# A fused decoder layer: its first projection taken 512 columns at a time, half of the weight remainders moved to GpSimd, and one softmax cut in two

## The chip, the cores and the metric

The kernel runs on one core of a Trainium2 chip. A time is the device time of one execution in microseconds (us). The engines are TensorE (PE; its weight loads are the row PEld), VectorE (DVE), ScalarE (ACT), GpSimd (POOL) and SyncE (SP), which here only issues DMAs. Each engine takes its instructions in program order and waits where an operand or a buffer is not ready.

## What is computed

One decoder layer over 256 tokens of width 2048, in float32:

```
xn = rms_norm(x);  proj = xn @ w_in                 # 2048 x 5696
o_nsa = gates * (compressed + selected + window attention)      # 16 heads
o_fox = attention with a forgetting bias                        # 16 heads
h = x + [rms_norm(o_nsa), rms_norm(o_fox)] @ w_out
h = h + sum over 32 experts of combine_e * (silu(hn@wg_e) * (hn@wu_e)) @ wd_e
out = rms_norm(h)
```

For the compressed branch, blocks of the projected columns `kcmp` and `vcmp` (512 columns together, called kcv here) go through a small MLP. Queries attend to the 15 blocks that come out.

## The kernel before

**Two parts.** For the first 470 us or so the core projects, attends, multiplies by `w_out` and routes. Then it streams the weights of all experts, 1 MB per DMA.

**Items.** `items` is the list of 1 MB weight blocks of the first part: 44 of `w_in`, then 16 of `w_out`. A block of `w_in` is 1024 rows by 256 columns, eight row chunks of 128, so two items make a projection of 256 columns. In order: kcv0, kcv1, v0, k0, v1, k1 (items 0 to 11), four query projections (12 to 19), then fq, fk and fv (20 to 43).

**hi and lo.** A product of float32 precision is made from rounded parts. `stream_conv(h)` splits half `h` of the items (two per item, 1024 elements per partition each): ACT writes `hi` (L190), then DVE writes `lo` = raw - hi (L191). The results lie in three buffers by turns, so half `h` can be split only when PE is done with half `h-3`. With `xh` and `xl` the parts of x, a projection takes `hi*xh`, `hi*xl` and `lo*xh`. `project` runs the first two as one matmul of 512 columns (`both`, or `xb(k)`), the third as one of 256, and adds the two accumulators at the end: an ACT copy (L321) and a DVE add (L322). `sum`, the result in SBUF, goes to `post`. The accumulators (`banks`, two PSUM banks each) are two by turns.

**The opening.** x arrives while items 0 and 1 (kcv0) run. Before chunk k the loop transposes block k+3 of x on PE (`x_chunk`, L294); ACT and DVE split it (L295, L296). From item 2 on `run_items` takes over.

**Background.** After each quarter of an item (two chunks) `run_items` makes one call of `background`: one step of the attention pipe, and one step of the first generator in `misc`. The generators of `misc` run in the order in which they were appended: `evac_kcv` (scales kcv into `kc2` with `row_scale`, L337), `gates`, then `compress`. `compress` first adds a vector to the blocks on POOL (`bk`, L481, 2 memsets and 8 adds), and in the same step starts the matmuls `bhc`. Later come `split_q_later` and `compressed`, once for each group of 8 heads. `compressed` makes `pcm`, the probabilities; four steps later PE transposes them (`bpt`, L744). `bpt` takes the PSUM bank that was used three takes before, by the scores `s_n` of an attention unit, so it waits until DVE has read those scores (L644).

Of the kernel before, what the change touches and what calls it, by code (L numbers as in the profile page):

```python
# [11 lines left out]
F32 = mybir.dt.float32  # L12
# [68 lines left out]
def tile_kernel(ctx: ExitStack, tc: tile.TileContext, a: dict, out):  # L81
# [33 lines left out]
    def mm(o, l, r, start, stop):  # L115
        pe.matmul(o, l, r, start=start, stop=stop, skip_group_check=True)  # L116
# [61 lines left out]
    def stream_conv(h):  # L178

        i, hf = divmod(h, 2)  # L180
        if i >= len(items):
            return
        nm, _, nk = items[i][:3]
        n2 = nk // 2
        cv = big.tile([P, n2, 2, 2048 // nk], F32R, tag=f"c{h % 3}", name=f"cv_{nm}_{hf}")
        hi, lo = cv[:, :, 0, :], cv[:, :, 1, :]
        r = raws[i][:, n2 * hf:n2 * hf + n2, :]
        n = n2 if h else n2 // 2
        for k in range(0, n2, n):
            act.activation(hi[:, k:k + n], r[:, k:k + n], AF.Copy)  # L190
            dve.tensor_tensor(lo[:, k:k + n], r[:, k:k + n], hi[:, k:k + n].bitcast(F32), ALU.subtract)  # L191
        halves[h] = cv

    def run_chunk(i, kk):
# [81 lines left out]
    def x_rows():  # L276
        for t in range(2):
            dve.tensor_scalar(oraw[0][:, 4, t * P:(t + 1) * P], ident, rsx[:, t:t + 1], None, ALU.mult)
        yield
        yield  # L280
        brs = bank("brs", "s")
        mm(brs[:, :T], onesq, oraw[0][:, 4, :], True, True)
        act.copy(rsb, brs[:, :T])
# [16 lines left out]
    def project(col, kind, name, post):  # L300
# [24 lines left out]
        for kg in range(2):  # L325
            items.append((f"{name}{kg}", w_in[kg * 1024:(kg + 1) * 1024, col:col + 256], 8,
                          lambda kk, hi, lo, both, kg=kg: chunk(kg, kk, hi, lo, both), end if kg == 1 else None))


    kc2 = []  # L330

    def row_scale(dst, src, f=None, s0=0):

        n, c, w = src.shape
        r = rsb[0:n, s0:s0 + w].unsqueeze(1).broadcast_to([n, c, w])
        if f is None:
            dve.tensor_tensor(dst, src, r, ALU.mult)  # L337
        else:
            dve.scalar_tensor_tensor(dst, src, f, r, ALU.mult, ALU.mult)

    def post_kcv(s_, i):
        kc2.append(ap_q.tile([P, 4, T], F32, tag="m6", name=f"kc2{i}", bufs=2))
        misc.append(evac_kcv(s_, i))
        if i == 1:
            misc.append(gates())
            misc.append(compress())

    def evac_kcv(s_, i):
        if i == 0:
            yield from x_rows()  # L350
            yield
            act.activation(w64h, w64, AF.Copy)
            dve.tensor_tensor(w64l, w64, w64h.bitcast(F32), ALU.subtract)
        yield
        kt = kc2[i]
        for gp in range(2):
            src = s_[64 * gp:64 * gp + 64]
            row_scale(kt[0:64, gp::2, :], src)
            row_scale(kt[64:128, gp::2, 0:T - 1], src[:, :, 1:T], s0=1)
            yield  # L360
# [192 lines left out]
    def pair_end(i, oT):  # L553

        if i < 8:
            G, j = divmod(i, 4)
            mm(oT[:, :T], vcbd[0][:, G, j, :], pTc[G], False, True)
        act.copy(oraw[i // 8][:, i % 8, :], oT[:, :T])
        part = i // 8
        if i % 8 == 0:  # L560
            pool.tensor_tensor(sq[:, part, :], oraw[i // 8][:, i % 8, :], oraw[i // 8][:, i % 8, :], ALU.mult)
        else:
            s2 = wk.tile([P, T], F32, tag="pcm", name=f"s2_{i}", bufs=1)
            pool.tensor_tensor(s2, oraw[i // 8][:, i % 8, :], oraw[i // 8][:, i % 8, :], ALU.mult)
            pool.tensor_tensor(sq[:, part, :], sq[:, part, :], s2, ALU.add)

# [139 lines left out]
    gb = gate.rearrange("p t (h b) -> p h t b", b=3)  # L706
    biases = {}

    def compressed(G, q):
        csc = bank(f"csc{G}", "s")  # L710
        for t in range(2):
            for r in range(4):
                o0 = (t * 4 + r) * 32
                mm(csc[:, o0:o0 + 32], q[:, r, t * P:(t + 1) * P],
                   kcd[:, 2 * G + r // 2].rearrange("p h c -> p (h c)"), t == 0 and r == 0, True)
        yield
        scs = wk.tile([P, 16, 16], F32, tag="scs", name=f"scs{G}", bufs=1)
        mx = wk.tile([P, 16], F32, tag="mx", name=f"mx{G}", bufs=1)
        ss = wk.tile([P, 16], F32, tag="ss", name=f"ss{G}", bufs=1)
        pcm = wk.tile([P, 2, P], F32, tag="pcm", name=f"pcm{G}", bufs=1)  # L720
        pool.memset(pcm, 0.0)
        scv = scs[:, :, 0:NBLK]
        for t in range(2):
            dve.tensor_tensor(scv[:, 8 * t:8 * t + 8],
                              csc[:, P * t:P * t + P].rearrange("p (u c) -> p u c", c=16)[:, :, 0:NBLK],
                              cb[:, t, 4 * G:4 * G + 4].rearrange("p r h c -> p (r h) c")[:, :, 0:NBLK], ALU.add)
        dve.tensor_reduce(mx, scv, AX.X, ALU.max)
        dve.tensor_scalar(mx, mx, -1e29, None, ALU.max)
        dve.tensor_tensor(scv, scv, mx.unsqueeze(2).broadcast_to([P, 16, NBLK]), ALU.subtract)
        yield  # L730
        act.activation(scv, scv, AF.Exp)
        yield
        dve.tensor_reduce(ss, scv, AX.X, ALU.add)
        dve.tensor_scalar(ss, ss, 1e-30, None, ALU.max)
        dve.reciprocal(ss, ss)
        dve.tensor_tensor(ss.rearrange("p (t h) -> p t h", t=2), ss.rearrange("p (t h) -> p t h", t=2),
                          gate.rearrange("p t (h b) -> p t h b", b=3)[:, :, 8 * G:8 * G + 8, 0], ALU.mult)
        dve.tensor_tensor(pcm.rearrange("p t (h c) -> p (t h) c", c=16)[:, :, 0:NBLK], scv,
                          ss.unsqueeze(2).broadcast_to([P, 16, NBLK]), ALU.mult)
        for _ in range(4):  # L740
            yield
        bpt = bank(f"bpt{G}", "s")
        for t in range(2):
            pe.transpose(bpt[:, t * P:(t + 1) * P], pcm[:, t], ident)  # L744
        pt = fp.tile([P, T], F32, name=f"pTc{G}")
        act.copy(pt, bpt[:, :T])
        pTc[G] = pt
        yield
# [11 lines left out]
    def post_q(s_, G, i):  # L760
        q = scaled
        evac_q(s_, q, i)
        if i == 0:
            qs2[G] = m8(f"m{2 + G}", f"q{G}", (4, 2, T), F32R)
            split_q(q, qs2[G], 0)
            return
        qs = qs2[G]
        misc.append(split_q_later(q, qs))
        misc.append(compressed(G, q))
        for j in range(4):  # L770
            p = 4 * G + j
# [280 lines left out]
    x_load(1024, D)  # L1052
    stream_dma(2)

    for i in range(2):
        post = items[i][4]
        if i:
            stream_dma(i + DMA_AHEAD)
        for kk in range(8):
            k = 8 * i + kk  # L1060
            if k == 0:
                x_chunk(0)
                x_chunk(1)
                stream_conv(0)
                x_chunk(2)
                stream_conv(1)
                stream_dma(3)
                sp.dma_start(csf, a["cst"][:, K_KEEP:K_W])
                early_loads()
            if k + 3 < 16:  # L1070
                x_chunk(k + 3)
            if k in (5, 8, 11, 13):
                n = (5, 8, 11, 13).index(k)
                square(n % 2, n // 2)
            if k == 14:
# [487 lines left out]
```

## Time and profile before

| | |
|---|---|
| time, median of 3 runs | 1428.51 us (1426.74 to 1428.99) |
| profiled execution | 1426.94 us, its span 1425.0 us |
| busy in the span | PE 1305.2 us (92%), DVE 510.8 (36%), ACT 328.3 (23%), POOL 80.0 (6%) |
| granted clock, mean | 0.991 |
| DMA | 479.94 MB, 337 GB/s over the span |

The clock is a share of full speed: 1.00 is the level of 2.4 GHz, 0.50 that of 1.2 GHz. Shares over the whole span mix two parts with different limits, so what a change in the first part does is read from that part.

### The profile page before, as it was taken

The page shows a single profiled execution, that of the slowest core. Times are in us where ns is not written, and L with a number is a line of the kernel's source. Part 1 is how long each engine was busy: PE and PEld are TensorE (multiplying, and loading weights), DVE is VectorE, ACT ScalarE, POOL GpSimd, SP SyncE. Part 2 cuts the span into 40 slices and gives each one's busy share as a digit, 9 for nine tenths or more (in the row PEclk, how much of TensorE's full clock was granted, in tenths as well). Part 3 has the DMA queues.
Part 4 walks back from the last instruction along what each step waited for, and adds up shares of the span by engine and source line. Part 5 has one row for each costly group of instructions (what it writes and reads, how often), then busy time and mean ns, then how long its engine had stood idle before and what let it go on. Part 6 is the DMA issues. An engine that isn't in the chain of part 4 may idle for free.

```text
span 1425.0 us, 16784 instructions
## 1 busy us (share of the span) xinstructions
PE 1305.2 (92%) x6758; PEld 733.7 (51%) x6758; DVE 510.8 (36%) x1013; ACT 328.3 (23%) x655; POOL 80.0 (6%) x95
## 2 busy tenths in 40 slices
PE   8999899999999999999998997997998899799885
PEld 6888688887787534334333442433433344243332
DVE  5656777767756304114113021220401212031022
ACT  5445556555545100100100000000000000000003
POOL 1200011131100003000000000000000000000003
PEclk9999999999999999999999999999999999999998
DMA  8655355655595899999999999999999999999994
GB/s 253 201 167 170 105 150 155 201 170 163 203 375 186 349 400 421 402 421 420 421 421 421 420 420 422 420 421 421 420 421 422 420 422 420 421 421 421 421 403 163
DMA packets 130772, 479.94 MB, mean 337 GB/s; under 512 B 14112, under 2 KB 69248, under 8 KB 82432
## 3 DMA queue, kind: packets, MB, share of 16 engines
q1 hardware_dynamic: 126320, 474.53, 85.0%
q10 hardware_dynamic: 4368, 4.27, 0.9%
q8 instruction: 55, 0.90, 0.3%
q14 instruction: 29, 0.24, 0.1%
HBM read 476.63 MB, written 2.14 MB: 336 GB/s over the span
## 4 chain that ended last, share of the span: by engine, by line
PE 50%; DMA 36%; DVE 7%; ACT 4%; issue 2%; SPq 0%; ACTq 0%; POOL 0%; DVEq 0%; POOLq 0%
DMA e_u<-in_expert_w_up_dram 14%; DMA e_d<-in_expert_w_down_dram 14%; PE bu L116 11%; DMA e_g<-in_expert_w_gate_dram 7%; PE bg L116 6%; PE wo L116 6%; PE by L116 6%; PE bo L116 3%; PE bx L116 2%; PE fq_ps L116 2%; PE fv_ps L116 2%; PE q_ps L116 2%; PE o L116 2%; PE v_ps L116 2%; PE fk_ps L116 2%
## 5 line engine op out<-in xcount | busy, mean ns | idle before, releaser
L116 PE MATMUL by<-e_d,hids 128*64 128x512 f32 (+2 forms) x1072 | 236.1, 576 | 32.5 <-DMA e_d<-in_expert_w_down_dram 31.8
L116 PE MATMUL bu<-e_u,xg 128*64 128x512 f32 x1024 | 242.4, 597 | 11.4 <-DMA e_u<-in_expert_w_up_dram 11.4
L116 PE MATMUL bg<-e_g,xg 128*64 128x512 f32 x1024 | 234.7, 596 | 12.7 <-DMA e_g<-in_expert_w_gate_dram 12.7
L1347 DVE TENSOR_TENSOR ys<-by,ys 128x512 fp32r<-128x512 f32 x60 | 40.0, 687 | 455.9 <-ACT ys L1346 455.1
L116 PEld LDWEIGHTS by<-e_d,hids 128*64 128x64 f32 x1072 | 79.9, 137 | 180.7 <-issue 117.1
L116 PEld LDWEIGHTS bg<-e_g,xg 128*64 128x64 f32 x1024 | 81.8, 137 | 142.9 <-issue 106.2
L116 PEld LDWEIGHTS bu<-e_u,xg 128*64 128x64 f32 x1024 | 78.7, 136 | 144.3 <-issue 112.7
L1361 DVE TENSOR_TENSOR y<-y,bo 128x512 f32<-128x512 f32 x112 | 71.9, 683 | 151.0 <-PE bo L116 151.0
L1346 ACT CAST ys<-by 128x512 fp32r<-128x512 f32 x60 | 35.2, 586 | 313.2 <-PE by L116 199.6
L116 PE MATMUL bo<-ys,scT 128*128 128x512 f32 x240 | 73.5, 427 | 13.3 <-ACT ys L1346 5.8
L116 PE MATMUL wo<-cv_wo,ohi 128*128 128x512 f32 x256 | 80.6, 396 | 0.0
L116 PEld LDWEIGHTS bx<-s,hh 128*128 128x128 f32 x512 | 63.7, 192 | 23.8 <-issue 13.0
L116 PE MATMUL bx<-s,hh 128*128 128x256 f32 x512 | 70.1, 290 | 4.6 <-DVE y L1361 2.9
L1275 DVE TENSOR_TENSOR xg<-bx,fw 128x512 f32<-128x512 f32 x64 | 43.5, 689 | 76.8 <-PE bx L116 76.8
L116 PEld LDWEIGHTS bo<-ys,scT 128*128 128x128 f32 x240 | 38.0, 188 | 60.1 <-issue 45.1
L1469 POOL TENSOR_TENSOR o<-y,e_fnw 128x256 f32<-128x256 f32 (+2 forms) x12 | 10.1, 866 | 836.2 <-DVE y L1382 836.2
L116 PEld LDWEIGHTS wo<-cv_wo,ohi 128*128 128x128 f32 x256 | 46.9, 188 | 10.4 <-issue 1.2
L1289 ACT CAST scT<-bsc 128x256 fp32r<-128x256 f32 x16 | 6.0, 372 | 193.8 <-PE bsc L116 193.8
L116 PE MATMUL fq_ps<-xhl,cv_fq 128*128 128x512 f32 (+1 forms) x256 | 50.5, 344 | 0.0
L1326 ACT COPY hids<-bh 128x512 f32<-128x512 f32 x16 | 9.4, 586 | 178.1 <-PE bh L1324 178.1
L116 PE MATMUL wo<-cv_wo,olo 128*128 128x512 f32 x128 | 50.0, 390 | 0.0
L1315 ACT ACTIVATE hids<-bg,c 128x512 f32<-128x512 f32 x16 | 11.0, 688 | 169.0 <-PE bg L116 169.0
(298 smaller groups left out, 1480.9 us busy)
## 6 DMA issues: line engine op xcount, KB each, us to landing
e_g<-in_expert_w_gate_dram SPq DMA_DIRECT2D x128, 1024.0 KB, 19.8
e_u<-in_expert_w_up_dram SPq DMA_DIRECT2D x128, 1024.0 KB, 19.8
e_d<-in_expert_w_down_dram SPq DMA_DIRECT2D x124, 1024.0 KB, 19.8
raw_wo<-in_w_out_dram SPq DMA_DIRECT2D x16, 1024.0 KB, 6.2
raw_q<-in_w_in_dram SPq DMA_DIRECT2D x8, 1024.0 KB, 5.3
raw_fq<-in_w_in_dram SPq DMA_DIRECT2D x8, 1024.0 KB, 5.2
raw_fk<-in_w_in_dram SPq DMA_DIRECT2D x8, 1024.0 KB, 5.2
raw_fv<-in_w_in_dram SPq DMA_DIRECT2D x8, 1024.0 KB, 5.3
```

Of the source, the lines that this page charges most:

```text
L116: pe.matmul(o, l, r, start=start, stop=stop, skip_group_check=True)
L1275: dve.tensor_tensor(xt_[:, i0:i0 + per, 0:m], bx.rearrange("p (i s) -> p i s", i=per), fw[:, 4 * j + i0:4 * j + i0 + per].unsqueeze(2).bro ...
L1289: act.copy(scT, bt[:, :T])
L1315: act.activation(hids[-1], bg_, AF.Silu, scale=c2[:, 1:2])
L1326: act.copy(hT, bh.rearrange("p (i s) -> p i s", i=4))
L1346: act.copy(hi, by[n])
L1347: dve.tensor_tensor(lo, by[n], hi.bitcast(F32), ALU.subtract)
L1361: dve.tensor_tensor(y[t][:, ns], base[t][:, ns], bo, ALU.add)
L1469: (dve if last else pool).tensor_tensor(o[t][:, ns], y[t][:, ns], fnw[:, ns], ALU.mult)
```

## The change

Three edits. (1) kcv is one projection of 512 columns (`project_first`): its items are 512 rows by 512 columns, four chunks each. Items 0 to 3 run inside the opening loop, one chunk per block of x. Each chunk takes 12 matmuls of 256 columns in place of 4 for half as many output columns. All three products add up in one accumulator, so the copy and the add at the end go away, and `evac_kcv` scales out of PSUM. (2) For the second half of each later item of `w_in` (`nk == 8`, 40 halves) `lo` is written on POOL. (3) `compressed` runs twice per group, for 4 heads each, the first half already after the group's first query projection. A buffer `s2` gets its own tag.

```diff
+        eng = pool if hf and nk == 8 else dve
         for k in range(0, n2, n):
             act.activation(hi[:, k:k + n], r[:, k:k + n], AF.Copy)
-            dve.tensor_tensor(lo[:, k:k + n], r[:, k:k + n], hi[:, k:k + n].bitcast(F32), ALU.subtract)
+            eng.tensor_tensor(lo[:, k:k + n], r[:, k:k + n], hi[:, k:k + n].bitcast(F32), ALU.subtract)
...
+    def project_first(col, name, post):
...
+            k = kg * 4 + kk
...
+            for ct in range(4):
+                o, cs = b[0][:, ct // 2, (ct % 2) * T:(ct % 2) * T + T], slice(ct * P, ct * P + P)
+                mm(o, hi[:, cs], xh(k), k == 0 and ct % 2 == 0, False)
+                mm(o, hi[:, cs], xl(k), False, False)
+                mm(o, lo[:, cs], xh(k), False, k == 15)
...
-    def post_kcv(s_, i):
-        kc2.append(ap_q.tile([P, 4, T], F32, tag="m6", name=f"kc2{i}", bufs=2))
-        misc.append(evac_kcv(s_, i))
-        if i == 1:
-            misc.append(gates())
-            misc.append(compress())
...
+    def post_kcv(b):
+        kc2.extend(ap_q.tile([P, 4, T], F32, tag="m6", name=f"kc2{i}", bufs=2) for i in range(2))
+        misc.append(evac_kcv(b))
+        misc.append(gates())
+        misc.append(compress())
...
+        for i in range(2):
+            kt = kc2[i]
+            for gp in range(2):
+                src = b[64 * gp:64 * gp + 64, i].rearrange("p (c t) -> p c t", c=2)
+                row_scale(kt[0:64, gp::2, :], src)
+                row_scale(kt[64:128, gp::2, 0:T - 1], src[:, :, 1:T], s0=1)
+                yield
...
-            s2 = wk.tile([P, T], F32, tag="pcm", name=f"s2_{i}", bufs=1)
+            s2 = wk.tile([P, T], F32, tag="s2", name=f"s2_{i}", bufs=1)
...
-    def compressed(G, q):
...
+    def compressed(G, q, i):
...
+        if i == 0:
+            return
...
+            misc.append(compressed(G, q, 0))
             return
         qs = qs2[G]
         misc.append(split_q_later(q, qs))
-        misc.append(compressed(G, q))
+        misc.append(compressed(G, q, 1))
...
-    for i in range(2):
+    for i in range(4):
         post = items[i][4]
         if i:
             stream_dma(i + DMA_AHEAD)
-        for kk in range(8):
-            k = 8 * i + kk
+        for kk in range(4):
+            k = 4 * i + kk
...
-            if kk % 4 == 0:
-                stream_conv(2 * i + 2 + kk // 4)
+            if kk % 2 == 0:
+                stream_conv(2 * i + 2 + kk // 2)
...
-    run_items(2, n_proj, at)
+    run_items(4, n_proj, at)
```

The order of the instructions before, on PE in the opening, from the transpose of block 3 of x on (`xt` are the transposes, `kcv_ps` the accumulator; chunks 0 and 1):

```order
L294 MATMUL xt_197<-cst,xs_85 128x128
L294 MATMUL xt_197<-cst,xs_86 128x128
L116 MATMUL kcv_ps<-xhl_114,cv_kcv_0_169 128x512
L116 MATMUL kcv_ps<-xhl_114,cv_kcv_0_169 128x256
L116 MATMUL kcv_ps<-xhl_114,cv_kcv_0_169 128x512
L116 MATMUL kcv_ps<-xhl_114,cv_kcv_0_169 128x256
L294 MATMUL xt_210<-cst,xs_85 128x128
L294 MATMUL xt_210<-cst,xs_86 128x128
```

And with the change, on PE at the same place:

```order
L295 MATMUL xt_197<-cst,xs_85 128x128
L295 MATMUL xt_197<-cst,xs_86 128x128
L116 MATMUL kcv_ps<-xhl_114,cv_kcv_0_169 128x256 x12
L295 MATMUL xt_218<-cst,xs_85 128x128
L295 MATMUL xt_218<-cst,xs_86 128x128
```

Between two pairs of transposes there are now 12 matmuls of 256 columns, where there were two of 512 and two of 256.

On POOL before, from the power that ends the norm of x (`rsx`) to the squares of the attention outputs (`sq`):

```order
L160 TENSOR_TENSOR rsx<-vx,neg_half 128x2
L1082 CAST lt<-csf 128x128
L1084 COPY fold<-cst 36x36 x2
L436 MEMSET gmem 16x127
L540 MEMSET kT_724 64x2048
L477 MEMSET bk 128x64
L481 TENSOR_TENSOR bk<-kc_352,vec 128x16x15 x4
L477 MEMSET bk 128x64
L481 TENSOR_TENSOR bk<-kc_451,vec 128x16x15 x4
```

On POOL with the change, from the fourth `lo` half (`cv_k`, item 7) to the one behind the adds:

```order
L192 TENSOR_TENSOR cv_k_1_649<-raw_k_498,cv_k_1_649 128x4x256
L192 TENSOR_TENSOR cv_v_1_732<-raw_v_546,cv_v_1_732 128x4x256
L455 MEMSET gmem 16x127
L559 MEMSET kT_760 64x2048
L192 TENSOR_TENSOR cv_v_1_794<-raw_v_600,cv_v_1_794 128x4x256
L496 MEMSET bk 128x64
L500 TENSOR_TENSOR bk<-kc_493,vec 128x16x15 x4
L496 MEMSET bk 128x64
L500 TENSOR_TENSOR bk<-kc_494,vec 128x16x15 x4
L192 TENSOR_TENSOR cv_k_1_872<-raw_k_692,cv_k_1_872 128x4x256
```

The eight `bk` adds stood behind nothing that waits for PE; now six `lo` halves stand ahead of them, the last of which (`cv_v_1_794`) is that of item 9.

On DVE with the change, from the `lo` of item 5's first half (`cv_v_0_500`) to the end of v0 (`v_sum`); `kc` is written from PSUM, and `cv_k_0_548` is the `lo` of item 6's first half:

```order
L192 TENSOR_TENSOR cv_v_0_500<-raw_v_349,cv_v_0_500 128x4x256
L279 TENSOR_SCALAR oraw_118<-cst,rsx 128x128 x2
L371 TENSOR_TENSOR w64hl<-gmem,w64hl 128x1024
L192 TENSOR_TENSOR cv_k_0_548<-raw_k_427,cv_k_0_548 128x4x256
L357 TENSOR_TENSOR kc_493<-kcv_ps,rsb 64x2x256
L357 TENSOR_TENSOR kc_493<-kcv_ps,rsb 64x2x255
L357 TENSOR_TENSOR kc_493<-kcv_ps,rsb 64x2x256
L357 TENSOR_TENSOR kc_493<-kcv_ps,rsb 64x2x255
L357 TENSOR_TENSOR kc_494<-kcv_ps,rsb 64x2x256
L357 TENSOR_TENSOR kc_494<-kcv_ps,rsb 64x2x255
L357 TENSOR_TENSOR kc_494<-kcv_ps,rsb 64x2x256
L357 TENSOR_TENSOR kc_494<-kcv_ps,rsb 64x2x255
```

All eight scalings now stand behind that `lo` half and read the accumulator `kcv_ps` itself; before, four stood one projection earlier, and all read a copy in SBUF.

## Rows read from the trace of the kernel before

**Rows 1.** Windows: us; then busy us of each engine, granted clock, DMA share, GB/s

```profile
core 0: us, PE busy (x) PEld busy (x) DVE busy (x) ACT busy (x) POOL busy (x), PEclk, DMA share, GB/s
8.50:27.75 19.25, 14.79 (x73) 12.28 (x73) 11.14 (x18) 12.68 (x23) 0.00 (x0) 0.82 1.03 294
27.75:42.44 14.69, 14.69 (x84) 12.70 (x84) 12.10 (x17) 8.75 (x13) 4.72 (x8) 1.00 0.73 224
...
128.24:160.00 31.76, 25.27 (x155) 21.77 (x154) 23.42 (x70) 17.20 (x43) 0.06 (x1) 0.89 0.42 125
160.00:300.00 140.00, 136.86 (x885) 116.08 (x884) 105.93 (x328) 83.86 (x213) 20.08 (x25) 1.00 0.53 162
300.00:400.00 100.00, 96.46 (x537) 78.78 (x537) 71.47 (x135) 51.96 (x98) 17.93 (x18) 1.00 0.57 190
```

**Rows 2.** The page's chain that ended last, shares of the span by line

```profile
DMA e_u<-in_expert_w_up_dram 14%; DMA e_d<-in_expert_w_down_dram 14%; PE bu L116 11%; DMA e_g<-in_expert_w_gate_dram 7%; PE bg L116 6%; PE wo L116 6%; PE by L116 6%; PE bo L116 3%; PE bx L116 2%; PE fq_ps L116 2%; PE fv_ps L116 2%; PE q_ps L116 2%; PE o L116 2%; PE v_ps L116 2%; PE fk_ps L116 2%
```

**Rows 3.** Timeline of PE in the opening: start, us, instruction, idle before, releaser

```profile
13.47 0.44 PE L294 MATMUL xt<-cst,xs 128*128 128x128 f32 x2 [1.64 <-DVE xhl L296]
...
16.45 0.69 PE L294 MATMUL xt<-cst,xs 128*128 128x128 f32 x2 [1.83 <-DVE xhl L296]
...
27.75 7.32 PE L116 MATMUL kcv_ps<-xhl,cv_kcv 128*128 128x512 f32 x40
...
42.44 5.82 PE L116 MATMUL v_ps<-cv_v,xhl 128*128 128x512 f32 x32
```

**Rows 4.** Timeline of PE at the experts' start, 16 matmuls of 256 columns

```profile
479.16 2.14 PE L116 MATMUL bx<-s,hh 128*128 128x256 f32 x16
```

**Rows 5.** The weights of v0: issue on SP's queue, and landing of the four

```profile
30.03 1.08 SPq L176 DMA_DIRECT2D raw_v<-in_w_in_dram  x2
...
DMA to landing us min/median/max: 5.4/7.6/10.3
```

**Rows 6.** One hi half on ACT (timeline), one lo half and one scaling on DVE (by form)

```profile
36.99 1.06 ACT L190 ACTIVATE cv_v<-raw_v 128x1024 fp32r<-128x1024 f32 x1
...
L191 DVE TENSOR_TENSOR cv_q<-raw_q,cv_q 128x1024 fp32r<-128x1024 f32 x16 | 19.4, 1222 | 7.1 <-ACT cv_q L190 7.0
L337 DVE TENSOR_TENSOR scaled<-k_sum,rsb 128x512 f32<-128x512 f32 x2 | 1.4, 692 | 0.1
```

**Rows 7.** POOL by form: adds and products of several widths, and the memsets of bk

```profile
L481 POOL TENSOR_TENSOR bk<-kc,vec 128x240 f32<-128x240 f32 x8 | 10.1, 1288 | 9.0 <-DVE kc L337 9.0
...
L1469 POOL TENSOR_TENSOR o<-y,e_fnw 128x512 f32<-128x512 f32 x4 | 5.0, 1278 | 831.4 <-DVE y L1382 831.4
L1469 POOL TENSOR_TENSOR o<-y,e_fnw 128x256 f32<-128x256 f32 x6 | 4.2, 727 | 4.5 <-DVE y L1382 4.5
...
L477 POOL MEMSET bk<- 128x64 f32 x2 | 0.5, 226 | 0.1
```

**Rows 8.** Timeline: first and last of the adds on POOL, PE around bhc

```profile
40.75 1.17 POOL L481 TENSOR_TENSOR bk<-kc,vec 128x240 f32<-128x240 f32 x1 [5.87 <-DVE kc L337]
...
51.10 3.07 POOL L481 TENSOR_TENSOR bk<-kc,vec 128x240 f32<-128x240 f32 x3 [1.34 <-DVE kc L337]
...
74.43 1.00 PE L116 MATMUL bcb<-tab,oh 128*128 128x64 f32 x8
75.24 1.64 PE L116 MATMUL v_ps<-cv_v,xhl 128*128 128x512 f32 x8
76.81 1.09 PE L116 MATMUL bhc<-oraw,bk 128*64 128x128 f32 x16
```

**Rows 9.** Timeline of POOL and DVE: a small DVE operation alone, and one beside POOL

```profile
132.69 0.17 DVE L648 TENSOR_SCALAR sm_n<-sm_n 128x4 f32<-128x4 f32 x1 [1.11 <-ACT pr_n L646]
...
256.10 1.30 POOL L794 TENSOR_TENSOR fb<-fb,csf 128x512 f32<-128x512 f32 x1
...
256.50 0.92 DVE L648 TENSOR_SCALAR sm_n<-sm_n 128x4 f32<-128x4 f32 x1 [1.11 <-ACT pr_n L646]
```

**Rows 10.** PE's longest wait (timeline), and windows of 1 us behind it

```profile
152.91 0.66 PE L744 MATMUL bpt<-cst,pcm 128*128 128x128 f32 x2 [6.49 <-DVE st_n L644]
...
154.00:155.00 1.00, 1.00 (x5) 0.89 (x4) 0.36 (x3) 1.00 (x5) 0.00 (x0) 0.50 0.05 16
155.00:156.00 1.00, 1.00 (x5) 0.85 (x4) 0.96 (x5) 1.00 (x3) 0.00 (x0) 0.69 0.00 0
156.00:157.00 1.00, 1.00 (x7) 0.86 (x6) 1.00 (x3) 0.23 (x1) 0.00 (x0) 1.00 0.00 0
```

More of the change, by code (lines that the diff above doesn't have):

```diff
@@ L327, in project, with chunk @@
                           lambda kk, hi, lo, both, kg=kg: chunk(kg, kk, hi, lo, both), end if kg == 1 else None))
+    def project_first(col, name, post):
+        b = []
+        def chunk(kg, kk, hi, lo, _):
+            k = kg * 4 + kk
+            if not b:
+                b.append(banks(f"{name}_ps"))
+            for ct in range(4):
[3 more added lines that the diff above has]
+                mm(o, lo[:, cs], xh(k), False, k == 15)
+        for kg in range(4):
+            items.append((f"{name}{kg}", w_in[kg * 512:(kg + 1) * 512, col:col + 512], 4,
+                          lambda kk, hi, lo, both, kg=kg: chunk(kg, kk, hi, lo, both),
+                          (lambda: post(b[0])) if kg == 3 else None))
     kc2 = []
@@ L339, in row_scale, with evac_kcv @@
             dve.scalar_tensor_tensor(dst, src, f, r, ALU.mult, ALU.mult)
-    def post_kcv(s_, i):
-        kc2.append(ap_q.tile([P, 4, T], F32, tag="m6", name=f"kc2{i}", bufs=2))
-        misc.append(evac_kcv(s_, i))
-        if i == 1:
-            misc.append(gates())
-            misc.append(compress())
[L348 to L353, printed above, removed]
-        yield
[L355 to L360, printed above, removed]
+    def post_kcv(b):
[3 more added lines that the diff above has]
+        misc.append(compress())
+    def evac_kcv(b):
+        yield from x_rows()
+        yield
+        act.activation(w64h, w64, AF.Copy)
+        dve.tensor_tensor(w64l, w64, w64h.bitcast(F32), ALU.subtract)
+        yield
[5 more added lines that the diff above has]
+                row_scale(kt[64:128, gp::2, 0:T - 1], src[:, :, 1:T], s0=1)
+                yield
     gate = fp.tile([P, 2, 48], F32, name="gate")
@@ L707, in tile_kernel @@
     biases = {}
-    def compressed(G, q):
-        csc = bank(f"csc{G}", "s")
+    pcms = {}
+    def compressed(G, q, i):
+        csc = bank(f"csc{G}{i}", "s")
         for t in range(2):
[L712 to L715, printed above, removed]
+            for r in range(2):
+                o0 = (t * 2 + r) * 32
+                mm(csc[:, o0:o0 + 32], q[:, 2 * i + r, t * P:(t + 1) * P],
+                   kcd[:, 2 * G + i].rearrange("p h c -> p (h c)"), t == 0 and r == 0, True)
         yield
[L717 to L721, printed above, removed]
+        if i == 0:
+            pcms[G] = wk.tile([P, 2, P], F32, tag="pcm", name=f"pcm{G}", bufs=1)
+            pool.memset(pcms[G], 0.0)
+        scs = wk.tile([P, 8, 16], F32, tag="scs", name=f"scs{G}{i}", bufs=2)
+        mx = wk.tile([P, 8], F32, tag="mx", name=f"mx{G}{i}", bufs=2)
+        ss = wk.tile([P, 8], F32, tag="ss", name=f"ss{G}{i}", bufs=2)
         scv = scs[:, :, 0:NBLK]
         for t in range(2):
-            dve.tensor_tensor(scv[:, 8 * t:8 * t + 8],
-                              csc[:, P * t:P * t + P].rearrange("p (u c) -> p u c", c=16)[:, :, 0:NBLK],
-                              cb[:, t, 4 * G:4 * G + 4].rearrange("p r h c -> p (r h) c")[:, :, 0:NBLK], ALU.add)
+            dve.tensor_tensor(scv[:, 4 * t:4 * t + 4],
+                              csc[:, 64 * t:64 * t + 64].rearrange("p (u c) -> p u c", c=16)[:, :, 0:NBLK],
+                              cb[:, t, 4 * G + 2 * i:4 * G + 2 * i + 2].rearrange("p r h c -> p (r h) c")[:, :, 0:NBLK],
+                              ALU.add)
         dve.tensor_reduce(mx, scv, AX.X, ALU.max)
         dve.tensor_scalar(mx, mx, -1e29, None, ALU.max)
-        dve.tensor_tensor(scv, scv, mx.unsqueeze(2).broadcast_to([P, 16, NBLK]), ALU.subtract)
+        dve.tensor_tensor(scv, scv, mx.unsqueeze(2).broadcast_to([P, 8, NBLK]), ALU.subtract)
         yield
@@ L735, in compressed @@
         dve.reciprocal(ss, ss)
[L736 to L739, printed above, removed]
+        sst = ss.rearrange("p (t h) -> p t h", t=2)
+        dve.tensor_tensor(sst, sst, gate.rearrange("p t (h b) -> p t h b", b=3)[:, :, 8 * G + 4 * i:8 * G + 4 * i + 4, 0],
+                          ALU.mult)
+        for t in range(2):
+            dve.tensor_tensor(pcms[G][:, t, 64 * i:64 * i + 64].rearrange("p (h c) -> p h c", c=16)[:, :, 0:NBLK],
+                              scv[:, 4 * t:4 * t + 4], sst[:, t].unsqueeze(2).broadcast_to([P, 4, NBLK]), ALU.mult)
+        if i == 0:
+            return
         for _ in range(4):
@@ L743, in compressed @@
         for t in range(2):
-            pe.transpose(bpt[:, t * P:(t + 1) * P], pcm[:, t], ident)
+            pe.transpose(bpt[:, t * P:(t + 1) * P], pcms[G][:, t], ident)
         pt = fp.tile([P, T], F32, name=f"pTc{G}")
@@ L844, in fkv @@
         return fox_mem(*(("m2", 1), ("m3", 0), ("m1", 0), ("m1", 1))[2 * G + hf])
-    for i in range(2):
-        project(C_KC + 256 * i, "T", f"kcv{i}", lambda s_, i=i: post_kcv(s_, i))
+    project_first(C_KC, "kcv", post_kcv)
     for br, col in enumerate((C_KS, C_KW)):
@@ L1053, in tile_kernel @@
     stream_dma(2)
-    for i in range(2):
+    for i in range(4):
         post = items[i][4]
```

## The prediction

> **What bounds the kernel now.** I read the page's chain first: behind the first part it consists of the experts' DMAs and PE alone [rows 2]. None of the three edits touches that part, and its stream starts when the first part is over. So a microsecond won or lost in the first part is one won or lost at the end, and I price the first part only. The windows by stage come next. In each, compare PE's busy time with the length of the window [rows 1]. From 27.75 to 42.44 us PE is busy for all of 14.69 us at clock 1.00: there only less PE work could help. It idles in the opening (8.50 to 27.75 us: 4.46 us idle, mean clock 0.82), where the queries' attention starts (128.24 to 160 us: 6.49 us idle, clock 0.89), and a little later on (160 to 400 us: 3.14 + 3.54 us). DVE is never full: 105.93 of 140 us. The timelines then say what ended PE's waits: in the opening the split of x on DVE [rows 3], later the reading of scores on DVE in front of `bpt` [rows 10].
>
> **Opening, a gain.** Before, PE waited 1.64 and 1.83 us for the split of x [rows 3], and a chunk brought only four matmuls between two such waits. ACT and DVE were busy 12.68 and 11.14 us in this window [rows 1], for nearly all blocks of x; with three more halves in the stage (1.06 and 1.22 us each, [rows 6]) they reach some 16 and 15 us, while PE now has all 16 chunks of 12 matmuls, about 25 us by the prices below. So PE becomes the slower of them. The idle 4.46 us go. So does the half clock: a mean of 0.82 over 19.25 us is 6.9 us at 0.50 [rows 1], of which PE could use all but some 0.5 us, so 3.2 us are lost to it. New waits: about 0.5 us each for the first two `lo` parts, 1.0 us in all. New work: the columns are the same, but 128 matmuls become 192. Alternating widths cost 7.32/40 = 0.183 us each [rows 3], so 23.4 us; widths of 256 cost 2.14/16 = 0.134 us at most [rows 4], so 25.7 us: +2.3, or down to 0 if the cost is by columns alone. I take +1.9. Sum: -4.5 - 3.2 + 1.0 + 1.9 = **-4.8 us** (bounds: -6.7 with no new cost, 0 if the waits only move and the clock stays down). Dropping ACT's copy and DVE's add at the end wins nothing more: PE did not wait for them.
>
> **v0's first weights, a loss.** v0 would start at 42.44 - 4.8 = 37.6 us. Its weights are issued at 30.03 us, behind small loads that do not change, and such a block lands 5.4 to 7.6 us later [rows 5], at 35.4 to 37.6. Add 1.06 for hi and 1.22 for lo [rows 6]: 37.7 to 39.9. **+0.8 us** (0 to 2.3).
>
> **Scaling out of PSUM, a loss.** k0 (item 6) takes the accumulator that kcv held, so its matmuls wait for the last of eight scalings. These stand on DVE behind the `lo` of item 6's first half, whose `hi` ACT cannot begin before PE has ended item 4. From there: 1.06 + 1.22 + 8 x 0.692 = 7.8 us [rows 6]. PE covers it with item 5, 32 matmuls in 5.82 us [rows 3]. **+2.0 us** (0 if DVE gets ahead; 4.4 if one GpSimd half holds it up). Before, a copy in SBUF freed the accumulator at once.
>
> **The adds of `bk`, the largest loss.** Before, POOL did them from 40.75 to 54.17 us, and PE came to `bhc` at 76.81 [rows 8]: 22 us of cover. Now they stand behind item 9's `lo` half, and that half waits until PE has ended the first half of item 8, since it needs that buffer. So the cover is gone. From that moment POOL's side takes 1.06 (hi, [rows 6]) + one `lo` half + 2 x 0.226 + 8 x 1.288 us [rows 7]. The `lo` half, 1024 elements, was never seen on POOL. From 727 ns for 256 and 1278 for 512 [rows 7] a line gives 2.38 us; twice the 512 gives 2.56; with a wait for DVE's 1.22 us it may be 3.6. I take 2.4, the line, being the nearest row to it. Sum 14.2 us. PE meanwhile has the second half of item 8 and the first of item 9, four groups of eight matmuls of 1.57 us (75.24 to 76.81), and two `bcb` of 0.81 us (74.43 to 75.24): 4 x 1.57 + 2 x 0.81 = 7.9 us [rows 8]. PE waits 6.3 us at `bhc` (5.4 with adds of 1.17, 7.5 with a slow `lo`). The wait of 6.49 us at `bpt` shows what follows one of that length: PE went on at 152.91 at clock 0.50, which rose to 1.00 between 155 and 156 us [rows 10]. That is some 2.8 us at half speed, 1.4 us lost. Together **+7.7 us** (5.4 to 9).
>
> Queued behind the adds: item 10's `lo` half, needed more than an item later, so covered. `gates` and `compress` run five background calls later in the list of items than before, since `evac_kcv` had eight calls in kcv1's place; their results are needed from item 11 on, by which they are done.
>
> **`bpt` and the attention, about nothing.** Here DVE loses two `lo` halves of 1.22 us ahead of the scores' reading, and half of the softmax has been done earlier. That would shorten the 6.49 us by up to 2.4, and PE by 1.4 us of half clock if the wait gets short. Against it stands what POOL does to DVE. A DVE operation of 0.17 us, begun 0.40 us into a POOL add of 1.30 us, took 0.92 us: it ended at 257.42, the add at 257.40 [rows 9]. So DVE was held to POOL's end, not slowed. A `lo` half on POOL of 2.4 us can then hold DVE for anything from 0 to 2.4 us; half of it, 1.2 us, is just what DVE saved. I take **0 us** for the 28 halves from the queries on. Bounds: -13.2 - 1.4 = -14.6 us if every idle microsecond from 128 to 400 us came back, and +15 us if DVE were held 0.5 us on the path for each of about 30 halves. Memsets and the split softmax cost a few operations of 0.2 us on DVE, hidden by its idle time.
>
> The Trainium skill, page "SBUF — State Buffer", section "Who interferes with whom", says that a VectorE instruction with two SBUF inputs, or in a two-port mode, and a GpSimd instruction that reads SBUF take the shared ports by an exclusive lock, for the whole instruction. The 0.92 us agree with that. By the rule alone each such DVE operation that meets a half waits for its end, so the sum would go up towards the +15 us; by the row, with half a length, it stays at 0.
>
> **The sum.** -4.8 + 0.8 + 2.0 + 7.7 + 0 = +5.7 us. On the profiled execution's own 1426.94 us that is 1432.6; its median of three runs is 1.6 us above it, so for a median I say **1434 us**.
>
> **The rivals.**
> - *GpSimd relieves DVE (faster).* If DVE's lighter queue gives back PE's later idle time, the limit is 14.6 us. Without that term the sum is +5.7, so it takes 8.6 us of it to come out faster by 0.2% (2.9 us, about what a measurement of this kernel can tell from no change). At 10 us: 1424. For it: the longest waits end on DVE. Against: the lock on small DVE operations [rows 9], and that `bpt` waits behind a ping-pong of ACT and DVE that stays. Chance 0.07.
> - *The adds get through (same).* If POOL does them in 0.73 us each, like other 256-element adds [rows 7], POOL's side is 9.8 us, PE's wait 1.9 us with no fall of the clock: the sum is -0.1, 1428.5. For it: same element count. Against: these adds took 1.17 us with DVE idle [rows 8]. With other mixes of small terms: chance 0.14.
> - *The lock decides (much slower).* DVE is held at each half, by the rule above: +5.7 + 10 to 15, so 1444 to 1449. For it: softmax steps are short operations in SBUF, all of the held kind. Against: DVE idles 34 of 140 us [rows 1]. Chance 0.17.
> - *The opening wins nothing* (clock stays low or matmuls of 256 are slow): 1439. Chance 0.10.
>
> **How the numbers follow.** My forecast, slower by 3 to 9 us, has 0.52. The predicted time is its middle. The range runs from the adds that get through, 1428, to the lower end of the lock, 1446: outside lie the relief of DVE (0.07) and the upper half of the lock (0.1). Slower: 0.52 + 0.17 + 0.10 = 0.79; same 0.14; faster 0.07.
>
> **What would show it.** v0's first matmul at 37 to 39 us and clock 1.00 from 8.5 us on (opening); a wait of PE for DVE's L357 in front of `k_ps` (scaling); a wait of 5.4 to 7.5 us in front of `bhc` put down to POOL, with clock 0.50 behind it; `lo` halves of 2.4 to 3 us on POOL; and `bpt` still waiting some 4 to 7 us. It is wrong if `bhc` does not wait, or if PE's idle time from 128 to 400 us changes by more than 5 us either way.

## The result, and the profile after

| | median | runs | ratio to before, 95% interval |
|---|---|---|---|
| before | 1428.6 us | 4 | |
| after | 1446.88 us (1444.42 to 1448.93) | 4 | 1.013 [1.0109, 1.0151] |

The change makes the kernel slower by some 18 us, 0.9 us above the top of my range (1428 to 1446). The profiled execution is the slowest of the four: span 1447.1 us, against 1425.0 before. So the trace shows 22.1 us where the medians show 18, and what follows divides these 22.1.

I cut the first part at four instants: the first matmul of v0, of the queries, of fq and of `w_out`. These are the windows between them in the trace of after; columns as in [rows 1].

```profile
core 0: us, PE busy (x) PEld busy (x) DVE busy (x) ACT busy (x) POOL busy (x), PEclk, DMA share, GB/s
8.50:36.44 27.94, 26.95 (x218) 25.97 (x219) 17.06 (x27) 18.80 (x33) 0.00 (x0) 1.00 0.93 287
36.44:108.70 72.26, 65.96 (x403) 55.28 (x404) 31.06 (x52) 28.66 (x38) 32.20 (x25) 0.93 0.53 160
108.70:175.85 67.15, 59.04 (x338) 50.98 (x337) 43.93 (x115) 36.46 (x73) 18.94 (x12) 0.90 0.47 142
175.85:377.90 202.05, 189.29 (x1166) 158.31 (x1165) 130.14 (x359) 108.17 (x255) 91.88 (x60) 0.97 0.49 153
```

And the same four stages in the trace of before, at its own instants:

```profile
8.50:42.44 33.94, 29.48 (x154) 24.98 (x155) 23.24 (x34) 21.43 (x35) 4.72 (x8) 0.90 0.90 263
42.44:103.40 60.96, 60.33 (x403) 51.33 (x402) 36.98 (x54) 27.00 (x36) 9.36 (x9) 1.00 0.58 174
103.40:166.20 62.80, 55.77 (x330) 48.21 (x329) 43.12 (x104) 36.06 (x71) 0.61 (x1) 0.95 0.50 151
166.20:356.00 189.80, 185.04 (x1175) 155.96 (x1174) 140.32 (x377) 108.69 (x255) 33.12 (x37) 1.00 0.53 163
```

Read the lengths first: -6.0, +11.3, +4.35 and +12.25 us. Behind `w_out`'s start nothing changes (1069.2 us to the end, 1069.0 before). Then take PE's busy time from the length. From v0 to the queries PE was idle for 0.63 us and now for 6.30; its 403 matmuls besides take 5.6 us longer, at clock 0.93. From fq to `w_out` idle time goes from 4.76 to 12.76 us, and 1166 matmuls take 4.3 us longer than 1175 did, at 0.97. So with the idle time the clock falls, and that costs about as much again in the second stage and half as much in the last.

What PE waits for, by the table of its waits from 6 to 400 us (us in total, times, longest):

```profile
PE bpt L772 <- DVE st_n L663: 10.4, 2, 7.4
PE o L116 <- DVE pT_f L629: 6.0, 2, 3.2
PE bhc L116 <- POOL bk L500: 3.3, 2, 2.3
PE t_f L626 <- DVE st_f L610: 2.7, 3, 1.6
PE k_ps L116 <- DVE kc L357: 2.6, 1, 2.6
```

PE hardly ever waits for POOL's `lo` halves themselves (0.4 us, once, in v0). What is late is DVE's softmax (`st_n`, `pT_f`, `st_f`). Its timeline shows why. First the compressed softmax of one half, then a `lo` half on DVE and the FoX softmax, each beside a `lo` half on POOL:

```profile
141.86 2.43 POOL L192 TENSOR_TENSOR cv_q<-raw_q,cv_q 128x1024 fp32r<-128x1024 f32 x1 [7.77 <-ACT cv_q L191]
142.05 0.35 DVE L747 TENSOR_TENSOR scs<-csc,cb 128x60 f32<-128x60 f32 x2
142.43 0.28 DVE L751 TENSOR_REDUCE mx<-scs 128x8 f32<-128x120 f32 x1
142.74 1.57 DVE L752 TENSOR_SCALAR mx<-mx 128x8 f32<-128x8 f32 x1
...
298.62 2.38 POOL L192 TENSOR_TENSOR cv_fq<-raw_fq,cv_fq 128x1024 fp32r<-128x1024 f32 x1
298.65 3.43 DVE L192 TENSOR_TENSOR cv_fq<-raw_fq,cv_fq 128x1024 fp32r<-128x1024 f32 x1 [0.27 <-ACT cv_fq L191]
...
313.80 2.35 POOL L192 TENSOR_TENSOR cv_fk<-raw_fk,cv_fk 128x1024 fp32r<-128x1024 f32 x1
313.85 2.33 DVE L616 TENSOR_SCALAR sm_f<-sm_f 128x2 f32<-128x2 f32 x1
```

Add start and duration. POOL's half ends at 144.29 us, L752 at 144.31: eight values per partition take 1.57 us, where 0.17 is usual. L616 begins 0.05 us behind a half of POOL and ends with it, after 2.33 us, on two values. The `lo` half that stayed on DVE at 298.65 takes 3.43 us: POOL's 2.38 and then its own time. L751, a reduction, and L747, which reads one of its inputs from PSUM, lie beside the same half and take what they always take.

### The profile page after: what moved, and what is told of

The parts are those of the page before. It is cut to its first block, busy times and chain, and to the rows that moved or that the text cites. A ratio compares the mean times of both kernels' runs of the same rounds, so it can differ in the third digit from the quotient of the medians.

```text
span 1447.1 us, 17002 instructions
## 1 busy us (share of the span) xinstructions
PE 1318.1 (91%) x6822; PEld 739.9 (51%) x6822; DVE 489.1 (34%) x995; ACT 326.8 (23%) x655; POOL 175.2 (12%) x135
## 4 chain that ended last, share of the span: by engine, by line
DMA 42%; PE 42%; DVE 7%; ACT 4%; issue 2%; SPq 1%; POOL 1%; ACTq 0%; DVEq 0%; POOLq 0%
DMA e_u<-in_expert_w_up_dram 15%; DMA e_d<-in_expert_w_down_dram 15%; DMA e_g<-in_expert_w_gate_dram 11%; PE bu L116 7%; PE wo L116 6%; PE bg L116 5%; PE by L116 5%; PE fv_ps L116 3%; PE bx L116 2%; PE bo L116 2%; PE fk_ps L116 2%; PE q_ps L116 2%; PE o L116 2%; PE k_ps L116 1%; PE fq_ps L116 1%
## 5 line engine op out<-in xcount | busy, mean ns | idle before, releaser
L116 PE MATMUL fk_ps<-xhl,cv_fk 128*128 128x512 f32 (+1 forms) x256 | 50.2, 347 | 0.0
L116 PE MATMUL q_ps<-xhl,cv_q 128*128 128x512 f32 (+1 forms) x256 | 49.9, 352 | 0.0
```

## The experiments

Four theories. **A**: while a GpSimd `lo` half runs, VectorE's operations in SBUF are held until it ends, and the chain behind them is late. **B**: the scalings, gates and `compress` stand later in the list, and what follows is shifted. **C**: the compressed softmax in two halves costs. **D**: PE waits for GpSimd's slower `lo` halves themselves. The stages of all kernels, from first matmul to first matmul, by their traces (us):

| kernel | start to v0 | v0 to queries | queries to fq | fq to w_out |
|---|---|---|---|---|
| before | 42.4 | 61.0 | 62.8 | 189.8 |
| after | 36.4 | 72.3 | 67.2 | 202.1 |
| opening alone | 37.7 | 66.2 | 63.0 | 189.2 |
| GpSimd alone | 41.3 | 70.3 | 64.3 | 196.7 |
| halves alone | 42.1 | 60.8 | 66.6 | 190.0 |
| opening + halves | 36.3 | 66.8 | 66.9 | 190.4 |
| after, GpSimd late | 37.4 | 66.1 | 66.8 | 201.7 |
| after, in pieces | 37.7 | 73.9 | 66.8 | 194.9 |
| before + idle GpSimd work | 42.3 | 71.0 | 67.8 | 210.3 |
| opening + copy | 37.4 | 61.4 | 63.2 | 189.5 |
| opening + copy + loads | 35.5 | 61.9 | 63.1 | 189.6 |

Each line is one trace. Three kernels that are alike up to v0 (opening alone, opening + halves, after with GpSimd late) come there at 36.3 to 37.7 us, so a difference of 1.4 us in the first column says nothing about a change.

**The opening alone.** The changed kernel with every `lo` on DVE and the compressed branch whole.

```diff
-        eng = pool if hf and nk == 8 else dve
+        eng = dve
...
```

> The first edit alone: kcv over 512 columns, all lo parts on DVE, the compressed softmax whole. Theory A (the lo halves on GpSimd hold DVE's SBUF operations and bring nearly all of the loss): v0 starts about 6 us earlier as in the changed kernel; the wait for the scaling out of PSUM stays, 2.6 us and 1.4 us of half clock, perhaps 1.2 us more for a second lo half between the scalings on DVE; no wait at bhc, since nothing stands ahead of the adds on GpSimd; bpt waits about 6.5 us as before. Sum -6.0 + 4.0 to 5.2: about 1427 us. Theory B (the later place of evac_kcv, gates and compress in the list of steps costs the time in the attention): 1434 us or more. Theory C (the split softmax costs it): as A.

Measured: 1427.85 us, ratio 1.0004 [0.9995, 1.0013]. The stage up to v0 gains 4.7 us, and the stage from v0 to the queries loses 5.2. PE's timeline of this kernel has two waits and what follows the second:

```profile
37.73 4.51 PE L116 MATMUL v_ps<-cv_v,xhl 128*128 128x512 f32 x24 [2.22 <-DVE cv_v L192]
...
53.39 2.31 PE L116 MATMUL k_ps<-xhl,cv_k 128*128 128x512 f32 x8 [3.78 <-DVE kc L357]
55.49 2.48 PE L116 MATMUL bgt<-xhl,w64hl 128*64 128x256 f32 x12
```

The first, for v0's weights, is already part of the 4.7. The second is the scaling out of PSUM, and what follows it runs partly at half clock: eight `k_ps` in 2.31 us (1.58 at full, below) and twelve `bgt` in 2.48 (1.53 in the kernel before). Together that is the 5.2, give or take 0.3. So edit 1 wins nothing as it stands, but it isn't what makes the kernel slower.

**GpSimd alone.** The kernel before with edit 2 from item 4 on.

```diff
+        eng = pool if hf and nk == 8 and i >= 4 else dve
...
-            dve.tensor_tensor(lo[:, k:k + n], r[:, k:k + n], hi[:, k:k + n].bitcast(F32), ALU.subtract)
+            eng.tensor_tensor(lo[:, k:k + n], r[:, k:k + n], hi[:, k:k + n].bitcast(F32), ALU.subtract)
```

> The second edit alone, from item 4 on: lo of the second halves on GpSimd, opening and softmax as before. Theory A: PE waits at bhc 2 to 5 us, DVE's small operations are held, and the stretch from the first fq matmul to the first w_out matmul grows by 10 to 13 us; the whole comes to 1443 to 1449 us. Theory B: no growth from fq on, 1433 us at most. Theory C: at most 1436 us. A fourth, D (PE waits for the lo halves themselves, which GpSimd makes late): as A in time, but PE's waits in front of projection matmuls are put down to GpSimd's lo, 5 us or more of them.

Measured: 1446.18 us, ratio 1.0139 [1.0123, 1.0154]: as large a loss as after's, from this one edit. Its waits on PE:

```profile
PE bpt L745 <- DVE st_n L645: 9.0, 2, 7.2
PE bhc L116 <- POOL bk L482: 6.3, 2, 4.2
...
PE o L116 <- DVE pT_f L611: 3.1, 2, 2.7
PE t_f L608 <- DVE st_f L592: 2.5, 3, 1.4
```

D falls: the table has no wait of PE for a `lo` half of GpSimd. B falls as the cause of the main loss. The time is where A had it, the parts are not: from fq to `w_out` the kernel loses 6.9 us, not 10 to 13, and the wait at `bhc` is 6.3 us, not 2 to 5.

**The halves alone.** The kernel before with edit 3 (the functions `compressed` and `post_q` of after).

```diff
...
+            misc.append(compressed(G, q, 0))
...
-        misc.append(compressed(G, q))
+        misc.append(compressed(G, q, 1))
```

> The third edit alone: the compressed softmax in two halves and the separate buffer, all else as before. Theory A: within 2 us of before, 1427 to 1430 us; bpt waits about 6 us. Theory C: 1433 us or more, with longer waits at bpt.

Measured: 1429.93 us, ratio 1.002 [1.001, 1.0029]. A small loss, most of it between the queries and fq (+3.8 us in the trace): PE busy there 59.15 us against 55.77, clock 0.92 against 0.95. Behind the wait for `bpt`, now 6.73 us and over at 152.61, PE's timeline goes on like this:

```profile
152.92 2.91 PE L116 MATMUL q_ps<-xhl,cv_q 128*128 128x512 f32 x8
155.63 1.75 PE L116 MATMUL csc<-kcd,scaled 128*128 128x32 f32 x8
157.19 2.91 PE L116 MATMUL q_ps<-xhl,cv_q 128*128 128x512 f32 x8
```

The second eight `q_ps` still run at half clock, where before the clock was back by 156 [rows 10]. That the extra `csc` between them keeps it down is likely, but no run shows it.

**Opening and halves, without GpSimd.** The one line of the first experiment's diff, on the changed kernel.

> The change without its second edit: opening over 512 columns and softmax in halves, all lo parts on DVE. Theory A: within 2 us of the first edit alone, about 1427 us, so some 20 us below the changed kernel. Theories B and C: 1434 us or more.

Measured: 1431.35 us, ratio 1.0035 [1.0021, 1.0048]. That is 3.5 us more than the first edit alone, where A allowed 2, and less than B and C asked for: the loss of edit 3 comes on top. So of after's 18 us, edits 1 and 3 together make about 5 (3 to 7 by the interval), and GpSimd's halves the other 13. Alone they cost some 20 (1.4%): the edits don't add up. Against this kernel's stages, after loses 5.5 us from v0 to the queries, 0.3 to fq, and 11.7 from fq to `w_out`.

**GpSimd late.**

```diff
-        eng = pool if hf and nk == 8 else dve
+        eng = pool if hf and i >= 20 and nk == 8 else dve
```

> The changed kernel with GpSimd's lower halves only from the FoX queries' weights on (items 20 and later); before that they are on VectorE. If GpSimd's subtractions cost time because VectorE's small steps are held while one runs, then the wait for the bk adds goes away (bhc 3.3 us to about 0, with its half clock), the first fq matmul is near the 170.0 us of the kernel with edits 1 and 3, and the stretch from there to the first wo matmul is still 9 to 13 us longer than the 190.4 us of that kernel: 1440 us (1437 to 1443). If it is the early place (scalings and bk adds) that shifts all that follows, the stretch is 190 to 192 us and the time 1431 to 1433 us.

Measured: 1442.89 us, ratio 1.0088 [1.007, 1.0106]. Up to fq the stages are those of the kernel without GpSimd (170.3 against 170.0 us), and from there it loses 11.4 us. The last stage of the kernel without GpSimd, and of this one, in windows:

```profile
170.00:360.36 190.36, 184.48 (x1167) 154.97 (x1166) 141.21 (x384) 108.21 (x255) 33.66 (x36) 1.00 0.53 163
```

```profile
170.30:372.04 201.74, 189.30 (x1167) 158.48 (x1165) 130.31 (x360) 108.19 (x255) 91.86 (x60) 0.97 0.50 153
```

PE and ACT have the same instructions (1167 and 255). DVE lost 24 `lo` halves, which took about 1.32 us each in the former kernel, 31.7 us. Its busy time fell by 10.9 only, so some 20 us went into longer instructions among those left on it (18.4 us if their durations are compared one group at a time). These are instructions from SBUF to SBUF. Those that read the scores in PSUM (`pr_n` from `s_n`) kept their time: over 256 columns 418 ns in the mean without GpSimd's halves and 416 with them. PE lost 6.6 us to waits and 4.8 to slower matmuls. Nothing early can be the cause here.

**GpSimd in pieces.**

```diff
-            eng.tensor_tensor(lo[:, k:k + n], r[:, k:k + n], hi[:, k:k + n].bitcast(F32), ALU.subtract)
+            m = n2 // 4 if eng is pool else n
+            for j in range(k, k + n, m):
+                eng.tensor_tensor(lo[:, j:j + m], r[:, j:j + m], hi[:, j:j + m].bitcast(F32), ALU.subtract)
```

> The changed kernel with each of GpSimd's lower halves cut in four subtractions of 256 elements (about 0.7 us each by [rows 7], some 2.8 us a half and so no less GpSimd time in all). If a VectorE instruction is held until the GpSimd instruction that runs has ended, the longest hold goes from 2.3 us to about 0.7 us and the loss shrinks: 1434 to 1441 us, with the mean of the small L752 and L758 steps under 0.9 us instead of 1.4. If what counts is GpSimd's total time, or that it keeps VectorE out as long as it has work, nothing shrinks: 1446 to 1450 us, and the small steps stay near 1.4 us.

Measured: 1442.64 us, ratio 1.009 [1.0073, 1.0107], a little above what A gave. From fq to `w_out` the loss over the kernel without GpSimd shrinks from 11.7 to 4.6 us, though GpSimd works longer (108.24 us busy there by its windows, against 91.88). The two small operations by form, in after, and then here, with two of their neighbours:

```profile
L758 DVE TENSOR_SCALAR ss<-ss 128x8 f32<-128x8 f32 x4 | 5.5, 1384 | 0.1
L752 DVE TENSOR_SCALAR mx<-mx 128x8 f32<-128x8 f32 x4 | 5.5, 1374 | 0.1
```

```profile
L754 DVE TENSOR_SCALAR mx<-mx 128x8 f32<-128x8 f32 x4 | 2.3, 584 | 0.1
L760 DVE TENSOR_SCALAR ss<-ss 128x8 f32<-128x8 f32 x4 | 0.7, 172 | 0.1
L755 DVE TENSOR_TENSOR scs<-scs,mx 128x120 f32<-128x120 f32 x4 | 2.6, 651 | 0.1
L766 DVE TENSOR_TENSOR pcm<-scs,ss 128x60 f32<-128x60 f32 x8 | 4.5, 602 | 0.3
```

So DVE is held to the end of one GpSimd instruction, not for as long as GpSimd has work. The holds got shorter, and more instructions meet one: L755 and L766 took 375 and 218 ns in after. No instruction in these four lines takes over 0.8 us now, where L752 and L758 had taken up to 1.97. The early stage, v0 to the queries, doesn't gain (73.9 us): there the adds of `bk` queue behind halves whose four pieces take 2.8 to 4.25 us, and PE waits 4.0 us for them.

**Idle work on GpSimd.** The kernel before; nobody reads what GpSimd computes in addition, and DVE does all it did.

```diff
+    scr = cp.tile([P, 512], F32, name="scr")
...
+        if hf and i >= 4 and nk == 8:
+            for k in (0, 2):
+                pool.tensor_tensor(scr.rearrange("p (k n) -> p k n", k=2), r[:, k:k + 2], hi[:, k:k + 2].bitcast(F32),
+                                   ALU.subtract)
```

> The kernel before, VectorE doing all lower halves as it did; GpSimd besides does two subtractions of 512 elements (about 1.28 us each) for each second half from item 4 on, into a tile that nobody reads. Nothing waits for their results. If the loss comes from GpSimd's activity holding VectorE, the kernel is slower by 10 us or more (1439 to 1450 us), and VectorE's small attention steps take over 1 us in the mean. If it came from lower halves that are ready later, or from the new order of VectorE's work, it is 1428 to 1430 us apart from the bk adds that queue behind them (at most +5, 1434 us).

Measured: 1463.29 us, ratio 1.024 [1.0223, 1.0257]. This is the strongest evidence for A, and more than I expected. First the page's busy times:

```profile
PE 1317.4 (90%) x6758; PEld 738.3 (50%) x6758; DVE 547.1 (37%) x1013; ACT 328.3 (22%) x655; POOL 219.7 (15%) x175
```

Then, by form, DVE's `lo` halves of the queries ([rows 6] has them at 1222 ns) and the added work beside them:

```profile
L192 DVE TENSOR_TENSOR cv_q<-raw_q,cv_q 128x1024 fp32r<-128x1024 f32 x16 | 25.6, 1617 | 2.5 <-ACT cv_q L191 2.5
...
L195 POOL TENSOR_TENSOR scr<-raw_q,cv_q 128x512 f32<-128x512 f32 x16 | 28.3, 1769 | 36.8 <-issue 35.1 <-POOL scr L195 1.1
```

The same 1013 DVE instructions took 36.3 us longer than before (510.8). GpSimd is held as well: 512 elements take 1769 ns, not 1278 [rows 7]. In one point I was wrong: the small steps (`mx`, `ss`) were not above 1 us in the mean but at 0.44 and 0.69. Of the 36.3 us some 15.5 fell on the `lo` halves, the rest mostly on scalings and softmax steps. Two reservations. From v0 to the queries, where 10.0 us are lost, PE waits 6.6 us for the `bk` adds that queue behind the idle work; the 25.5 us lost from the queries to `w_out` hold no wait of PE for GpSimd. And the extra work keeps `raw` and `hi` in use for longer, which can delay a conversion; PE's waits for halves of the queries come to 1.4 us (0.8 for DVE, 0.6 for ACT; 0.5 before), so that is a small part.

**Opening and copy.** Edit 1 alone, with a copy of kcv into SBUF as soon as it is done.

```diff
-        misc.append(evac_kcv(b))
+        act.copy(scaled.rearrange("p a b -> p (a b)"), b.rearrange("p a b -> p (a b)"))
+        misc.append(evac_kcv(scaled.rearrange("p (i c) t -> p i (c t)", i=2)))
```

> Edit 1 alone, and ScalarE copies the 512 columns of the first projection from PSUM into SBUF as soon as they are done; the scalings read the copy. If the opening's 6 us are lost again because the second K projection waits for the scalings to free PSUM, that 3.8 us wait and the half clock behind it go: 1423.5 to 1426 us. If the wait only turns up at the next tensor (v0's weights, bk adds, bpt), it stays at 1427 to 1428.5 us.

Measured: 1423.49 us, ratio 0.9956 [0.9942, 0.997], faster than both kernels. The copy costs ACT 0.99 us. PE's timeline has no wait in front of `k_ps`, and full speed in it:

```profile
49.88 1.58 PE L116 MATMUL k_ps<-xhl,cv_k 128*128 128x512 f32 x8
```

**Opening, copy, and the small loads later.**

```diff
-                early_loads()
...
+        if i == 1:
+            early_loads()
```

> The kernel with edit 1 and the copy, and the early small loads (gate weights, offsets' table, second-layer weights) issued behind the first 1024 KB of v0's weights and not ahead of them. If v0's weights were late because these small loads stood ahead of them in the queue, the first v_ps matmul comes at 36 us instead of 37.4, with no wait of 2.2 us for its lower part: 1420 to 1422 us. If the gate weights are then late in their turn, or a buffer is what is waited for, there is no gain beside the copy alone: 1423 to 1425 us.

Measured: 1422.52 us, ratio 0.9957 [0.9943, 0.9971]. The wait for v0's weights is gone and the first v_ps comes at 35.52 us. But the trace of opening + halves, which has the loads where they were, shows no such wait either, so this one trace doesn't show that the loads were the cause. The span is 1.2 us shorter than with the copy alone (spans 1420.4 and 1421.6), but the two ratios can't be told apart, so its gain stays unclear.

## Why the prediction was wrong, point by point

By stage, the forecast was -4.0 up to v0, +9.7 to the queries and 0 to `w_out`; the traces have -6.0, +11.3 and +16.6 us.

**Bounds and stages: right.** What is lost before `w_out` starts is lost at the end; the stage behind it is unchanged to 0.2 us.

**Opening and v0, forecast -4.8 + 0.8.** Right in the mechanism, and better than forecast: v0 begins 6.0 us earlier, at 36.44 us and not at 37 to 39, and the clock is 1.00 from 8.5 us on. The new matmuls were priced too high: 48 of them take 6.00 us behind the last transposes, so 192 take 24.0 us, 0.6 more than before and not 1.9. The trace after shows little wait for the weights of v0 (0.68 us, then 0.39); with the opening alone it was 2.22 us, at the end of the bounds.

**Scaling out of PSUM, forecast +2.0.** Right mechanism, too small. The wait is 2.63 us in after and 3.78 with the opening alone, and I priced no half clock behind it. In opening + halves, where the wait is 3.67 us, the stage from v0 to the queries is 5.8 us longer than before, for +2.0 foreseen. The copy experiment removed the wait and its price, and gave 4.8 us of that stage back (66.2 to 61.4), which shows the cause.

**The adds of `bk`, forecast +7.7.** Right mechanism, too large: PE waits for POOL in front of `bhc`, 3.3 us in after, where I had 6.3 (5.4 to 7.5), and the clock falls behind it. With GpSimd alone it is 6.3. After costs 5.5 us in this stage over opening + halves, GpSimd alone 9.3 over before. The `lo` half took 2.35 to 2.53 us, as estimated. The adds were the wrong term. I wrote that one had taken 1.17 us "with DVE idle", but DVE was busy with scalings from SBUF at the time:

```profile
39.92 2.55 DVE L337 TENSOR_TENSOR kc<-kcv_sum,rsb 64x510 f32<-64x510 f32 x3
```

That lasts until 42.47 us, and the add ran from 40.75 to 41.92 [rows 8]. In after the last six of the eight adds, with nothing of DVE beside them, took 0.72 us each, and all eight 6.9 us instead of my 10.3. With that the sum gives a wait of 2.9 us. So the ground of the rival "the adds get through" held for the adds, and what was left of the wait still came.

**"`bpt` and the attention, about nothing": the step that failed.** It cost 16.6 us, 4.35 from the queries to fq and 12.25 from there to `w_out`. About 4 of the first are edit 3: its split softmax was called hidden, but the half clock behind `bpt` lasts longer with it. 11.7 of the second come with GpSimd's halves, from the holds and the half clock behind PE's waits, against bounds of -14.6 and +15 of which I took the middle. I had the right row, [rows 9], and read it rightly: held to POOL's end. The error was to net 1.2 us held against 1.2 us of DVE time saved. The time saved was on `lo` halves that PE mostly didn't wait for; the time held fell on softmax steps that it did wait for, and on the `lo` halves that stayed. "DVE idles 34 of 140 us" was no argument against it either: the holds lie on a serial chain, not in DVE's idle time. PE's idle time from the queries to `w_out` grew from 11.8 to 20.9 us, past the 5 us that I had named as a sign of being wrong. And not every softmax step is "of the held kind": L751 and the steps that read PSUM are not. The Trainium skill, page "SBUF — State Buffer", section "Who interferes with whom", lists which VectorE instructions compete with GpSimd (tensor_scalar in two-port modes, anything with two SBUF inputs against a GpSimd instruction that reads SBUF) and which on trn2 never do (tensor_reduce). The rows agree: L752 at 1.57 us and L751 at 0.28 us, both beside the same half of POOL. In which mode L752 ran, no row shows.

So the rival "the lock decides", 1444 to 1449 us, is what happened, and edit 2 alone shows it as well as the three together. A is shown, for the larger part of the loss, by four runs that go against B, C and D: edit 2 alone brings as large a loss, late halves keep the late part of it, short instructions shrink it, and work that nobody waits for makes it larger. What stays open is the exact split. GpSimd alone loses 9.3 us from v0 to the queries and 6.9 from fq to `w_out`; with edits 1 and 3 it is 5.5 and 11.7. Where a hold lands depends on small shifts that I didn't trace one by one.

## What to carry to other kernels

Work given to GpSimd isn't free because nobody waits for it: list which VectorE operations in SBUF will run beside it and stand on the path, and charge each with up to one GpSimd instruction; if work must go there, cut it in short instructions (here that got back 4 of the 18 us). Time saved on an engine counts where the critical chain waits for it, so it can't be set off against time lost on that chain. When a projection is merged, keep an early copy out of PSUM: that 1 us on ScalarE turned a gain of zero into one of 0.44%.

## What the hardware showed that I had not expected

GpSimd's own time depends on VectorE. The eight adds of 240 elements took 1288 ns in the mean before, 890 in after and 711 with GpSimd in pieces. In after, POOL's two groups of four adds, and two DVE instructions with both inputs in SBUF beside the first group:

```profile
77.64 2.39 DVE L551 TENSOR_TENSOR kT<-scaled,kT 64x512 fp32r<-64x512 f32 x1 [1.33 <-ACT kT L550]
79.52 4.11 POOL L500 TENSOR_TENSOR bk<-kc,vec 128x240 f32<-128x240 f32 x4
80.43 1.27 DVE L192 TENSOR_TENSOR cv_k<-raw_k,cv_k 128x1024 fp32r<-128x1024 f32 x1
...
83.67 2.70 POOL L500 TENSOR_TENSOR bk<-kc,vec 128x240 f32<-128x240 f32 x4
```

A subtraction of 512 elements took 1769 ns beside DVE's halves, where a product of 512 was seen at 1278. Each side pays for the other. And a wait of a few microseconds on TensorE costs more than itself: in the last stage of the late-GpSimd kernel 6.6 us of waits came with 4.8 us of slower matmuls.
